# First stage of a two-layer diffusion backbone: pinning TensorE's order and rearranging what the pooling mixer waits for

## The chip, the cores and the metric

The kernel runs on one core of a Trainium2 chip. The metric is the device time of one execution in microseconds (us), as the median of several runs; lower is better. Engines are named as in the profile: PE is TensorE (matmuls), PEld its weight loads, DVE is VectorE, ACT is ScalarE, POOL is GpSimd, and SP is SyncE, which issues all the loads here. "Lnnn" is a line of the kernel before.

## The reference, cut to what matters

Two layers work on 512 latent tokens and 256 context tokens of width 1024, all in float32. Layer 0 mixes tokens by pooling, layer 1 by attention; each is followed by a squared-ReLU MLP with an inner width of 4096. Only the first half of layer 0 matters here:

```python
m = silu(cond) @ w_ada[i] + b_ada[i]             # 6 x 1024: sh1, sc1, gt1, sh2, sc2, gt2
h = rms_norm(x, g_mix_pre) * (1 + sc1) + sh1     # the context has its own conditioning vector
# pool_mixer, group g of four, window w = 2, 4, 8, 16 tokens
diff = mean_over_window(h) - h                   # the constant sh1 falls out of this difference
y    = concat(diff_g @ w_pool[g]) * pool_scale
x    = x + gt1 * rms_norm(y, g_mix_post)
h2   = rms_norm(x, g_mlp_pre) * (1 + sc2) + sh2
x    = x + gt2 * rms_norm(relu(h2 @ w_in) ** 2 @ w_out, g_mlp_post)
```

## The kernel before, in words

Matrix products are made in three passes of split operands: a "hi" copy rounded to the fp32r type and a "lo" remainder (hi·hi, hi·lo, lo·hi). So whatever enters a product has an ACT instruction that writes hi and a DVE instruction that writes lo. Tokens stand in six tiles of 128 rows: t = 0 to 3 latent, 4 and 5 context. Channels stand in eight blocks of 128: k = 0 to 7, two for each pooling group.

The first stage ends where the product of layer 0's `w_mlp_in` block 0 (`psin`, from tile `rb`) is done and that of block 1 (`psin` from tile `units`, L530) begins. It does the following.

1. SP issues the small `vecs` loads (L185, L186), the six row tiles and the band matrices (L189, L191), and then one block of 1 MB after another: twenty blocks of `w_ada` for layer 0 in the order of the list `CONDITIONING`, and `w_pool`. `raw_load` (L106 to L111) puts a block into a tile of a pool: `rawe` with four buffers unless another pool is given. SP waits until a buffer is free, and `keep_in_program_order` keeps the `raw_load`s in their order.
2. Row tiles: a mean square on ACT (L155), a power on POOL (L170), scaled rows on DVE (L314).
3. Pooling as a band matrix: `band_mm` (L394) multiplies rows by a band and writes the transposed difference of mean and row to PSUM, latent tokens in `psm`, context tokens in `psc`. `band_ev` (L405) copies blocks k = 0 to 3 to SBUF tiles `stage` of the pool `rawp` (three buffers); k = 4 to 7 stay in PSUM.
4. Conditioning: `ada_mm` (L200 to L211) multiplies the silu vector by a pair of blocks (w = 4, 512 columns) or one block (w = 2, 256 columns) on PE (L208) and transposes the result on DVE (L210). `ada_sel` (L218) sums it on PE (L215) and writes `mods` and `avec` on DVE (L226, L235). A buffer of `rawe` is free after L208, or, for the second block of a pair, after L215, because the transposed result is written into the block itself.
5. `centred(k)` (L422 to L433): the modulated difference, in hi and lo. It needs the shift and the scale of its blocks.
6. `pool_weights` (L441) loads `w_pool` into a `rawe` buffer and the scale row into a `rawp` tile, multiplies them on DVE (L446), and `split` (L124) makes hi and lo on ACT (L127) and DVE (L130).
7. `pool_a(t)` (L450): 24 matmuls into a PSUM tile of two banks from `psA`, which has two such tiles. `gate_rows` (L279) spreads the gate over the partitions on PE (L284) and copies it on ACT (L286). `pool_ms`, `pool_b` (L307), `norm_r` (L310), `norm_s`, `norm_c` make the residual and the scaled rows. `turn0`, `mod0` (L355 to L377) transpose and modulate them, and `parts0` runs `psin`.

Two things set the order. Each piece is put on a list with a planned time (`st.at(time, fn, ...)`, L690 to L737), and the list, sorted, gives the program order. The scheduler then orders each engine's instructions by its own estimate of when each is ready, with program order as priority, except for those in `keep_in_program_order`. On the chip each engine runs its instructions in the order that results. In the kernel before, no PE instruction of this stage is kept in program order.

## Time and profile before

| | |
|---|---|
| time, three runs | median 1180.1 us (1179.85 to 1182.94) |
| the profiled execution's own time | 1181.59 us |
| its span | 1179.8 us |
| PE busy over the span | 1143.2 us (97%) |
| DVE, ACT busy over the span | 941.9 us (80%), 639.2 us (54%) |
| mean granted TensorE clock | 0.993 |
| first product of block 1 (end of the first stage) | 111.08 us |

The span runs from the first instruction of the program to the last; the time holds 1.8 us more around it. A row of the timeline gives start, length, engine, line, operation, written<-read tiles, the number of instructions merged into it, and in brackets the idle time before it with what ended it. A row of the groups gives the number of instructions, the busy time and the mean in ns of one. A row of the stretches gives begin and end, length, then each engine's busy time and instructions, the granted TensorE clock as a share, the DMA engines' busy share and GB/s.

### The profile page before, as it was taken

What the parts mean: (1) busy time and instruction counts of PE and PEld (TensorE: products, weight loads), DVE (VectorE), ACT (ScalarE), POOL (GpSimd) and SP (SyncE); (2) the same over time, 40 slices, a digit from 0 to 9 for tenths busy, and PEclk for the clock granted to TensorE, in tenths of its full rate; (3) what the DMA queues carried; (4) which work ended last, traced back from release to release, by engine and by line L of the source; (5) the groups of instructions that cost most, each with busy time, mean ns of one, the idle gap of its engine ahead of it and who ended that gap; (6) DMA issues with size and microseconds to landing.
All of it is one profiled execution on the core that took longest, in us unless ns stands there. A gap on an engine that the chain in (4) does not pass through costs nothing.

```text
span 1179.8 us, 15965 instructions
## 1 busy us (share of the span) xinstructions
PE 1143.2 (97%) x6168; PEld 989.3 (84%) x6168; DVE 941.9 (80%) x1543; ACT 639.2 (54%) x1087; POOL 68.9 (6%) x120
## 2 busy tenths in 40 slices
PE   6799999999999999999999999999899999999997
PEld 4479989899889988998887889998888888888886
DVE  3777777989988999897687589977687779778876
ACT  3667654545444455554576377863676346535522
POOL 2030000000000000000131210001100000000001
PEclk9899999999999999999999999999999999999999
DMA  8986113443333343334521200105234124314212
GB/s 339 339 303 228 42 69 110 143 143 143 144 143 129 121 143 143 107 120 151 194 72 61 83 1 37 37 34 200 109 126 175 42 102 143 108 36 143 107 32 111
DMA packets 25658, 147.84 MB, mean 125 GB/s; under 512 B 2800, under 2 KB 5232, under 8 KB 9840
## 3 DMA queue, kind: packets, MB, share of 16 engines
q1 hardware_dynamic: 25584, 146.84, 34.6%
q8 instruction: 48, 0.79, 0.3%
q14 instruction: 26, 0.21, 0.1%
HBM read 139.49 MB, written 7.34 MB: 124 GB/s over the span
## 4 chain that ended last, share of the span: by engine, by line
PE 49%; issue 42%; DVE 3%; POOL 3%; ACT 2%; DMA 1%; SPq 0%; POOLq 0%; DVEq 0%; ACTq 0%
PE pso L758 22%; PE psin L654 18%; PE psin L530 3%; PE psq L1005 2%; PE pspool L457 2%; PE psada L208 1%; POOL rs L170 1%; ACT junk L155 1%; POOL rs L1014 1%; DMA xr<-in_x 1%; DVE xr L310 0%; PE psc L400 0%; PE psx L360 0%; DVE rows L250 0%; DVE ra L433 0%
## 5 line engine op out<-in xcount | busy, mean ns | idle before, releaser
L758 PE MATMUL pso<-units,rb 128*128 128x512 f32 x1152 | 278.2, 392 | 0.0
L758 PEld LDWEIGHTS pso<-units,rb 128*128 128x128 f32 x1152 | 214.8, 188 | 41.2
L250 DVE SCALAR_TENSOR_TENSOR rows<-raw,cond,rows 128x256 f32<-128x256 f32 x280 | 126.5, 477 | 2.0
L770 DVE TENSOR_TENSOR acc<-acc,pso 128x512 f32<-128x512 f32 x129 | 85.1, 675 | 40.8 <-PE pso L758 40.7
L530 PE MATMUL psin<-ra,rb 128*128 128x512 f32 (+1 forms) x432 | 104.0, 341 | 2.3 <-ACT ra L345 1.6
L862 PE MATMUL pso<-units,pairs 128*128 128x512 f32 x336 | 82.3, 389 | 0.0
L530 PEld LDWEIGHTS psin<-ra,rb 128*128 128x128 f32 x432 | 70.0, 189 | 12.6 <-ACT ra L345 1.9
L530 PE MATMUL psin<-ra 128*128 128x512 f32 x256 | 80.5, 389 | 0.0
L862 PEld LDWEIGHTS pso<-units,pairs 128*128 128x128 f32 x336 | 63.1, 188 | 13.1
L866 DVE TENSOR_TENSOR acc<-acc,pso 128x512 f32<-128x512 f32 x72 | 48.7, 683 | 28.5 <-PE pso L862 28.5
L168 POOL TENSOR_SCALAR ms<-ss 128x1 f32<-128x1 f32 x20 | 9.6, 480 | 1004.2 <-ACT junk L155 992.1
L654 PE MATMUL psin<-ra,units 128*128 128x384 f32 x336 | 65.6, 337 | 0.4 <-ACT psin L666 0.4
L654 PE MATMUL psin<-sums,units 128*128 128x384 f32 x336 | 63.9, 337 | 0.0
L654 PEld LDWEIGHTS psin<-ra,units 128*128 128x128 f32 x336 | 59.8, 188 | 4.0 <-ACT psin L666 0.9
L654 PEld LDWEIGHTS psin<-sums,units 128*128 128x128 f32 x336 | 58.9, 188 | 1.6
L130 DVE TENSOR_TENSOR units<-raw,units 128x1024 fp32r<-128x1024 f32 (+2 forms) x49 | 55.2, 1149 | 5.0 <-ACT units L127 4.9
L530 PEld LDWEIGHTS psin<-ra 128*128 128x128 f32 x256 | 48.0, 188 | 10.0
L768 ACT COPY acc<-pso 128x512 f32<-128x512 f32 x48 | 27.1, 587 | 50.0 <-PE pso L758 49.6
L127 ACT CAST units<-raw 128x1024 fp32r<-128x1024 f32 (+2 forms) x49 | 46.9, 994 | 13.2 <-PE pso L758 9.3
L530 PE MATMUL psin<-rb 128*128 128x512 f32 (+1 forms) x144 | 52.8, 367 | 0.2 <-DVE rb L346 0.2
L1005 PE MATMUL psq<-units,ra 128*128 128x512 f32 x216 | 51.7, 392 | 0.0
L530 PE MATMUL psin<-rb,ra 128*128 128x512 f32 x128 | 49.8, 389 | 0.0
(252 smaller groups left out, 2357.3 us busy)
## 6 DMA issues: line engine op xcount, KB each, us to landing
raw<-in_w_ada SPq DMA_DIRECT2D x48, 1024.0 KB, 5.3
raw<-in_w_mlp_in SPq DMA_DIRECT2D x32, 1024.0 KB, 4.9
raw<-in_w_mlp_out SPq DMA_DIRECT2D x32, 1024.0 KB, 5.3
raw<-in_w_qkv SPq DMA_DIRECT2D x6, 1024.0 KB, 4.9
spill<-xr SPq DMA_DIRECT2D x10, 512.0 KB, 6.2
xr<-spill SPq DMA_DIRECT2D x10, 512.0 KB, 7.8
raw<-in_w_o SPq DMA_DIRECT2D x4, 1024.0 KB, 5.0
xr<-in_x SPq DMA_DIRECT2D x4, 512.0 KB, 5.3
```

Of the source, the lines that this page charges most:

```text
L127: a = sc.copy(hi, raw)
L130: b = ve.tensor_tensor(out=lo, in0=raw, in1=hi, op=ALU.subtract)
L250: ve.scalar_tensor_tensor(out=r, in0=raw[:, k, :], scalar=cond[:, k, c:c + 1], in1=r, op0=ALU.mult, op1=ALU.add)
L457: te.matmul(pss[g // 2][:, (g % 2) * 256:(g % 2 + 1) * 256], a[:, k, sl], b[:, k, :], start=(n == 0), stop=(n == len(seq) - 1))
L530: te.matmul(ps[:, bank, o:o + ln], w[:, k, fs], rhs, start=start, stop=(k == KT - 1 and n == 2), skip_group_check=len(ks) < KT)
L654: te.matmul(bank, w[k], a[k], start=start and k == 0 and m == 0, stop=stop and k == 3 and m == 2, skip_group_check=True)
L758: te.matmul(pss[h][:, 0:cols[h][1]], a[:, f, ts_], w[:, f, cols[h][0]:sum(cols[h])], start=(n == 0 and not seeded[t]), stop=(n == len(seq) ...
L768: sc.copy(d, ps)
L770: ve.tensor_tensor(out=d, in0=d, in1=ps[:, 0:w], op=ALU.add)
L862: te.matmul(ps, a, w, start=(m == 0), stop=(m == len(seq) - 1))
L866: ve.tensor_tensor(out=M[n][:, t], in0=M[n][:, t], in1=ps, op=ALU.add)
L1005: te.matmul(ps, a[:, k, sl], w[:, k % 4, :], start=(k == 0 and n == 0), stop=(k == KT - 1 and n == 2))
```

## The change

It does six things, all in the first stage.

- **Order of PE.** A wrapper `Kept` around TensorE puts every PE instruction issued between the planned times 0 and 50.4 into `keep_in_program_order`. The planned times of the stage are set anew: `ada_mm` and `ada_sel` get a time each in place of one time and one more.
- **`vec`** is loaded after the rows instead of before them.
- **Pool weights.** `w_pool` goes to the pool `rawp`, not to a `rawe` buffer. The scale row is loaded in two halves into the unused 512 columns of the two `stage` tiles, and the multiplication is made in two halves (`pool_scaled`).
- **`centred` in two passes.** hi = scale·difference + 0 on ACT, lo = scale·difference − hi on DVE, straight from the difference. The separate product plus shift, and its subtraction, go. `minus` becomes a tile of zeros, computed as `mods − mods`, so that it still depends on the shift.
- **Mixer by groups.** `pool_a` can run some of the four groups: tiles 4 and 5 run groups 0 and 1, 2, and 3 at separate places, and tile 4 uses two one-bank tiles of the pool `psB` (four banks) instead of a `psA` tile.
- **Blocks of `band_mm`.** Blocks k = 4, 5 and 6, 7 go in pairs, latent tokens first.

```diff
+class Kept:
+    def __init__(self, tc, engine, on):
+        self.tc, self.engine, self.on = tc, engine, on
+    def __getattr__(self, name):
+        f = getattr(self.engine, name)
+        if not self.on[0]:
+            return f
+        return lambda *args, **kw: self.tc.keep_in_program_order(f(*args, **kw))
...
-    sy, ve, sc, gp, te = nc.sync, nc.vector, nc.scalar, nc.gpsimd, nc.tensor
+    ordered = [False]
+    sy, ve, sc, gp, te = nc.sync, nc.vector, nc.scalar, nc.gpsimd, Kept(tc, nc.tensor, ordered)
...
         if (i, m) == (0, SH1):
-            ve.tensor_scalar(out=minus[:, 2 * j:2 * j + w], in0=mods[i][:, at:at + w, 0:nc_], scalar1=-1.0,
-                             scalar2=None, op0=ALU.mult)
+            ve.tensor_tensor(out=minus[:, 2 * j:2 * j + w], in0=mods[i][:, at:at + w, 0:nc_],
+                             in1=mods[i][:, at:at + w, 0:nc_], op=ALU.subtract)
...
     def centred(k):
-        pm, w = means.pop(k), work_tile()
+        pm = means.pop(k)
         for ci, (t0, ln) in enumerate(SEGS):
-            z, hi, lo = w[:, t0:t0 + ln], hH[:, k, t0:t0 + ln], hL[:, k, t0:t0 + ln]
+            hi, lo, m = hH[:, k, t0:t0 + ln], hL[:, k, t0:t0 + ln], pm[ci][:, 0:ln]
             sa = avec[0][0][:, k, ci:ci + 1]
-            b = mods[0][:, SH1 * KT + k, ci:ci + 1]
-            if ci == 0:
-                sc.activation(z, pm[ci][:, 0:ln], AF.Identity, scale=sa, bias=b)
-            else:
-                ve.tensor_scalar(out=z, in0=pm[ci][:, 0:ln], scalar1=sa, scalar2=b, op0=ALU.mult, op1=ALU.add)
-            sc.activation(hi, z, AF.Identity, bias=minus[:, k, ci:ci + 1])
-            ve.scalar_tensor_tensor(out=lo, in0=z, scalar=b, in1=hi, op0=ALU.subtract, op1=ALU.subtract)
+            sc.activation(hi, m, AF.Identity, scale=sa, bias=minus[:, k, ci:ci + 1])
+            ve.scalar_tensor_tensor(out=lo, in0=m, scalar=sa, in1=hi, op0=ALU.mult, op1=ALU.subtract)
...
     def pool_weights():
-        wraw = raw_load(w_pool)
-        pscale = rawp.tile([P, 2048], F32, tag="raw", name="pscale")[:, 0:D]
-        sy.dma_start(pscale, pool_scale[0].partition_broadcast(P))
+        wraw = raw_load(w_pool, rawp)
         w4 = wraw.rearrange("p (g k n) -> p g k n", k=2, n=256)
-        ve.tensor_tensor(out=w4, in0=w4, in1=pscale.rearrange("p (g n) -> p g n", n=256).unsqueeze(2)
-                         .broadcast_to([P, 4, 2, 256]), op=ALU.mult)
-        pw.append((wraw, wpH, wpL))
-
-    def pool_a(t):
+        for h, (_, spare) in enumerate(stage.values()):
+            sy.dma_start(spare, pool_scale[0, 512 * h:512 * h + 512].partition_broadcast(P))
+        pw.extend((wraw, wpH, wpL))
...
+    def pool_a(t, gs=range(4), small_banks=False):
+        if t not in mix:
+            if small_banks:
+                mix[t] = [psB.tile([P, 512], F32, tag="b", name="pspool") for _ in range(2)]
+            else:
+                pp_ = psA.tile([P, 2, 512], F32, tag="a", name="pspool")
+                mix[t] = [pp_[:, 0, :], pp_[:, 1, :]]
         sl = slice(t * P, (t + 1) * P)
-        pp_ = psA.tile([P, 2, 512], F32, tag="a", name="pspool")
-        pss = [pp_[:, 0, :], pp_[:, 1, :]]
-        for g in range(4):
+        for g in gs:
...
-    landing = (15.3, 20.3, 26.2, 28.6, 31, 33.4, 39.5, 44.3, 49, 53.5, 58.5, 61, 63.4, 65.8)
-    for z, (m, j, w) in zip(landing, CONDITIONING):
-        ada_at(st, z, 0, m, j, w)
+    landing = ((19.5, 23.6), (21.5, 25.4), (28.4, 29.7), (30, 31.2), (32.5, 33.6), (35.2, 37.2), (42, 44.5), (47.2, 49.4),
+               (51, 53.2), (55.5, 57.6), (60.5, 61.7), (62.9, 64), (65.2, 66.4), (67.7, 68.8))
+    for (z, zs), (m, j, w) in zip(landing, CONDITIONING):
+        st.at(z, ada_mm, 0, m, j, w)
+        st.at(zs, ada_sel, 0, m, j)
+    st.at(0, ordered.__setitem__, 0, True)
+    st.at(50.4, ordered.__setitem__, 0, False)
...
-    for t in range(NT):
-        st.at(8 + 1.3 * t, band_mm, t, range(4))
+    for t, z in enumerate((8.6, 9.9, 11.3, 13, 14.6, 18.4)):
+        st.at(z, band_mm, t, range(4))
...
+    for k in (4, 6):
+        z = 16.1 if k == 4 else 23.4
+        st.at(z - 0.1, band_open, k)
+        for t in range(NL):
+            st.at(z + t / 10, band_mm, t, (k, k + 1))
+        for t in range(NL, NT):
+            st.at((25.6 if k == 4 else 27) + t / 10, band_mm, t, (k, k + 1))
     for k in range(KT):
-        st.at([22, 23.5, 25, 26.5, 30.2, 31.7, 35, 36.2][k], centred, k)
-    st.at(21.5, pool_weights)
-    st.at(27.5, lambda: split(*pw[0]))
+        st.at([26.4, 27.5, 28.6, 29.6, 32.2, 33.2, 38.2, 39.2][k], centred, k)
+    st.at(23, pool_weights)
+    st.at(25.3, pool_scaled)
+    st.at(30.5, lambda: split(*pw))
...
-            st.at((40.9, 45.7)[h] + (0.1, 0)[ci], gate_rows, 0, GT1, ci, (h,))
+            st.at((44.8, 49.6)[h] + (0.1, 0)[ci], gate_rows, 0, GT1, ci, (h,))
     order = (4, 5, 0, 1, 2, 3)
+    st.at(34.5, pool_a, 4, (0, 1), True)
+    st.at(36.7, pool_a, 4, (2,))
+    st.at(37.8, pool_a, 5, (0, 1, 2))
+    st.at(40.4, pool_a, 4, (3,))
+    st.at(40.5, pool_a, 5, (3,))
     for n, t in enumerate(order):
-        b = 46.4 + 3 * n
-        st.at((36.4, 39.8, 46.8, 49.8, 52.8, 55.8)[n], pool_a, t)
+        b = 50.5 + 2.9 * n
+        if n > 1:
+            st.at((44.9, 52.6, 55.6, 58.4)[n - 2], pool_a, t)
```

The planned times after these (`pool_ms`, `turn0`, `mod0`, `parts0`, the load of `w_mlp_in`) move later by 1.0 to 4.1 us.

More of the change, by code (lines that the diff above doesn't have):

```diff
@@ L185, in backbone @@
     sy.dma_start(given, vecs[:, 160:176])
-    sy.dma_start(vec, vecs[:, 0:160])
     xt = x.rearrange("b (t p) d -> p (b t) d", p=P)
@@ L193, in backbone @@
         xload(t)
+    sy.dma_start(vec, vecs[:, 0:160])
     sc.activation(cond[:, :, 0:2].rearrange("p k c -> p c k"), given.rearrange("p (c k) -> p c k", k=KT),
@@ L406, in band_ev @@
         if k not in stage:
-            stage[k] = rawp.tile([P, 2048], F32, tag="raw", name="stage")[:, 0:2 * TOK].rearrange("p (u n) -> p u n", n=TOK)
+            z = rawp.tile([P, 2048], F32, tag="raw", name="stage")
+            stage[k] = z[:, 0:2 * TOK].rearrange("p (u n) -> p u n", n=TOK), z[:, 2 * TOK:]
         t0, ln = SEGS[q]
-        (sc.copy if on_act else ve.tensor_copy)(stage[k][:, :, t0:t0 + ln], (lat, con)[q][k])
+        (sc.copy if on_act else ve.tensor_copy)(stage[k][0][:, :, t0:t0 + ln], (lat, con)[q][k])
         if q:
             for u in range(2):
-                means[k + u] = [stage[k][:, u, t0:t0 + ln] for t0, ln in SEGS]
+                means[k + u] = [stage[k][0][:, u, t0:t0 + ln] for t0, ln in SEGS]
     rs, mix, yg, first = {}, {}, {}, []
@@ L712, in backbone @@
[L712 to L713 removed]
+        st.at([26.4, 27.5, 28.6, 29.6, 32.2, 33.2, 38.2, 39.2][k], centred, k)
+    st.at(23, pool_weights)
+    st.at(25.3, pool_scaled)
+    st.at(30.5, lambda: split(*pw))
     raws = []
[L715 to L716 removed]
+    st.at(56.5, lambda: first.append(Inner(0, w_in(0, 0, ring, False, raws), hH, hL, hids0[0], chunks0, TOK)))
```

31 lines of the change are left out of this document (14 added, 17 removed).

## The prediction, made before the changed kernel was run

> **What bounds the kernel now.** I read the busy times by stretches first, then PE's waits, SP's issues and landings, and the timeline of PE and DVE in the stretch with the idle time.
>
> ```profile
> 0.00:28.60 28.60, 19.67 (x136) 14.58 (x136) 9.22 (x20) 11.49 (x18) 7.61 (x18) 1.00 0.89 336
> 28.60:44.60 16.00, 7.62 (x93) 3.27 (x89) 14.67 (x29) 11.93 (x19) 0.00 (x0) 0.75 0.99 367
> 44.60:65.60 21.00, 19.18 (x165) 13.69 (x161) 11.67 (x28) 8.88 (x20) 1.72 (x4) 0.86 0.91 340
> 65.60:111.20 45.60, 44.39 (x421) 37.94 (x418) 35.11 (x60) 31.85 (x61) 12.41 (x20) 1.00 0.67 245
> 111.20:150.00 38.80, 38.80 (x203) 35.87 (x202) 30.98 (x42) 28.04 (x40) 0.00 (x0) 1.00 0.22 80
> ```
>
> Columns: stretch, length, PE, PEld, DVE, ACT, POOL busy, granted clock, DMA share, GB/s. From 65.6 on PE is the bound: 44.39 of 45.6 us, then 38.8 of 38.8. So the kernel gains what the first stage lets PE reach earlier. The idle time lies before: 8.4 us of 16 from 28.6 to 44.6, where DVE is busy for 14.67 us, and the clock is 0.75 there and 0.86 in the next stretch.
>
> ```profile
> PE psada L208 <- DMA raw<-in_w_ada: 4.1, 2, 3.6
> PE psada L215 <- DVE mods L226: 3.4, 1, 3.4
> ```
>
> In this stretch (waits of PE, 26 to 45 us) PE waits for a block of `w_ada`, then, at L215, for DVE. Why is that block late?
>
> ```profile
> 1.63 0.42 SPq L189 DMA_DIRECT2D xr<-in_x  x1
> 4.95 2.82 SPq L108 DMA_DIRECT2D raw<-in_w_ada  x4
> 22.23 0.33 SPq L108 DMA_DIRECT2D raw<-in_w_pool  x1
> 26.50 23.32 SPq L108 DMA_DIRECT2D raw<-in_w_ada  x9
> raw<-in_w_ada SPq DMA_DIRECT2D x1, 1024.0 KB, 10.1
> raw<-in_w_ada SPq DMA_DIRECT2D x1, 1024.0 KB, 15.0
> pscale<-in_pool_scale SPq DMA_DIRECT2D x1, 512.0 KB, 13.9
> raw<-in_w_pool SPq DMA_DIRECT2D x1, 1024.0 KB, 7.7
> raw<-in_w_ada SPq DMA_DIRECT2D x1, 1024.0 KB, 6.6
> ```
>
> The last column of the DMA rows is us from issue to landing: for the first and fourth of the four early blocks (issued at 4.95 and 7.44), for the scale row (11.28), `w_pool` (22.23) and the next `w_ada` (26.50). So blocks land at 15.05 and 22.44, (22.44 − 15.05) / 3 = 2.46 us each; scale row and gains at 25.2; `w_pool` only at 29.9, because its `rawe` buffer came free at 22.2; the next `w_ada` at 33.1, where PE's wait ends.
>
> **The change part by part.** I follow PE up to the gate.
>
> ```profile
> 8.63 6.11 PE L400 MATMUL psm<-gate,acc 128*128 128x136 f32 x32 [8.63 <-DVE acc L314]
> 15.03 1.19 PE L400 MATMUL psc<-gate,acc 128*128 128x136 f32 x8 [0.30 <-DVE acc L314]
> 16.06 3.02 PE L400 MATMUL psm<-gate,acc 128*128 128x136 f32 x24
> 48.39 1.90 PE L208 MATMUL psada<-raw,cond 128*32 128x512 f32 x16
> 59.38 0.25 PE L215 MATMUL psada<-raw,sel 128*32 128x8 f32 x8 [1.22 <-DVE raw L210]
> 50.36 0.72 DVE L210 STREAM_TRANSPOSE raw<-psada 128x512 f32<-128x512 f32 x1 [0.48 <-PE psada L208]
> 53.64 0.23 DVE L273 TENSOR_TENSOR gc<-mods,vec 128x4 f32<-128x4 f32 x2
> 53.30 1.22 PE L457 MATMUL pspool<-rb,ra 128*128 128x256 f32 x8
> 54.36 1.95 PE L284 MATMUL psg<-ident,gc 128*128 128x128 f32 x16
> 60.21 3.45 PE L284 MATMUL psg<-ident,gc 128*128 128x128 f32 x16 [0.58 <-DVE gc L273]
> 63.69 0.58 ACT L286 COPY gate<-psg 128x512 f32<-128x512 f32 x1 [1.12 <-PE psg L284]
> 65.60 6.01 PE L457 MATMUL pspool<-rb,ra 128*128 128x256 f32 x48
> ```
>
> *`vec` behind the rows* frees one SP issue ahead of them: the rows' first issue moves from 1.63 to 1.16, and all that follows with it, PE's start at 8.63 too: 0.47 us. The `w_ada` blocks behind `vec` gain less; I take 22.2 for the fourth.
>
> *PE's order up to 25.7.* Tile 4 starts at 15.03 − 0.47 = 14.6 and ends at 15.8; 16 instructions for k = 4, 5 at 3.02 / 24 = 0.126 take 2.0, tile 5 takes 1.2: 19.0. Then the first pair, 1.9: 20.9. The second pair's first half, 0.95, ends at 21.85, its second waits for 22.2: 23.15. The latent k = 6, 7, 2.0: 25.2; two sums at 0.25: 25.7. Scale and shift are there at about 26.5 and `centred` begins, against 30.04 (first L429) before. The bands of the context fill PE until 28.1.
>
> *Pool weights out of `rawe`.* SP issues `w_pool` right behind the fourth block: 22.2 + 2.5 = 24.7. Scale row and gains took 25.2 − 22.44 = 2.8 before and are still there: 27.5. The first `rawe` buffer comes free at 19.9, halfway through the first pair, and goes to `w_ada` at once; the next at 21.85 and, behind the two sums, about 25.5. So the next four blocks land at 30.0, 32.4, 34.9 and 37.4, against 33.1 and on: three us earlier. If the scale's halves went behind a `w_ada` block, they would land 2.5 later; DVE has `centred` to do meanwhile, so I count nothing. The Trainium skill, "DMA: Bandwidth & Descriptors", section Bandwidth, has a rule that speaks against this part: transfers should be of 1 MiB or more, and the halves have a quarter of that. By the fixed 2.0 us that the page puts on each transfer, the scale would be about 2 us later, an estimate; the trace shows landings 2.46 us apart in a queue of blocks, with no such gap between them, and the sum stays either way, as `centred` fills DVE.
>
> *`centred` in two passes, and DVE's sum.* The next bound is DVE:
>
> ```profile
> L433 DVE SCALAR_TENSOR_TENSOR ra<-work,mods,ra 128x512 fp32r<-128x512 f32 x8 | 6.0, 745 | 0.1
> L433 DVE SCALAR_TENSOR_TENSOR ra<-work,mods,ra 128x256 fp32r<-128x256 f32 x8 | 3.7, 469 | 0.0
> L431 DVE TENSOR_SCALAR work<-psc,avec,mods 128x256 f32<-128x256 f32 x4 | 2.0, 538 | 0.0
> L431 DVE TENSOR_SCALAR work<-stage,avec,mods 128x256 f32<-128x256 f32 x4 | 1.5, 406 | 0.0
> L446 DVE TENSOR_TENSOR raw<-raw,pscale 128x2048 f32<-128x2048 f32 x1 | 2.3, 2284 | 0.0
> L130 DVE TENSOR_TENSOR rb<-raw,rb 128x2048 fp32r<-128x2048 f32 x2 | 4.6, 2292 | 0.0
> L210 DVE STREAM_TRANSPOSE rows<-psada 128x256 f32<-128x256 f32 x8 | 3.5, 442 | 0.6 <-PE psada L208 0.5
> L226 DVE TENSOR_TENSOR mods<-psada,vec 128x4 f32<-128x4 f32 x8 | 1.2, 155 | 3.2 <-PE psada L215 3.1
> L307 DVE TENSOR_TENSOR acc<-pspool,gate 128x512 f32<-128x512 f32 x12 | 7.8, 682 | 8.8 <-ACT gate L286 5.0 <-ACT junk L155 3.8
> L429 ACT ACTIVATE work<-psm,mods,avec 128x512 f32<-128x512 f32 x4 | 2.9, 773 | 6.5 <-DVE mods L226 6.5
> ```
>
> Gone are the eight of L431, 4 × 0.538 + 4 × 0.406 = 3.8 us of DVE, and the eight of L429 on ACT, 8 × 0.79 = 6.3 us, which were not the bound. Left from 26.5 on: 16 lo's, 8 × (0.745 + 0.469) = 9.7; scaling 2.28; split 2.29; four transposes 1.77; eight small ones 1.25: 17.3 us, so DVE is through at 43.8 if nothing starves it. The last conditioning needed, at 37.4, is then no bound. A lo with its source in PSUM has no row; by L307, which reads PSUM, a 512 one lies near 0.68, by L433 at 0.745, so 16 of them change the sum by under 0.6; I keep L433.
>
> *Mixer by groups.* The same 24 instructions for a tile, at 6.01 / 48 = 0.125. Only the last group of tiles 4 and 5, 12 × 0.125 = 1.5, is left after 43.8: 45.3. Before, these tiles ended at 53.30 + 1.22 = 54.5: 9.2 earlier. Two banks of `psB` are held until `pool_b`; two are left for conditioning and gate, which go one after another. Nothing by that, and up to one gate copy, 0.58, if they collide.
>
> *From there to the gate, pinned.* The first gate pair (in by 42.4) 1.9: 47.2; transpose 0.72, sum 0.25, `mods` and gate column 0.155 + 0.23: 48.6; `psg` 1.95: 50.5; `pool_a(0)` 24 × 0.125 = 3.0: 53.5; second pair (in by 47.4) 55.4; the same 1.37: 56.8; `psg` 58.7; second gate copy about 59.5, against 63.69 + 0.58 = 64.3. The scheduler can put the first SC2 pair, 1.9, under the copies: PE is at 60.9 where it was at 65.6, with `pool_a(0)` done besides. In this walk PE stands idle for two transposes, sums and small ones, 2 × 1.1 us; nothing ready may pass a pinned instruction.
>
> *After 60.9* the same work is left less 3.0 us: 45.6 − 3.0 = 42.6, so the stage ends at 103.5 in place of 111.2. The blocks of SC2 and SH2 come some 11 us earlier than before by the same chain of buffers, so they don't bound it; DVE has 35.1 us of work in it and ACT 31.9, still under 42.6. The gain is (65.6 − 60.9) + 3.0 = **7.7 us**. The profiled execution, 1181.6, becomes 1173.9; it lies 1.5 over the median of 1180.1, which becomes **1172.4**.
>
> **The rivals.**
>
> *A. The stream of blocks sets the end.* DVE gets through sooner (small ones under other waits, the split early), and the gate follows its block. Then the second gate pair at 47.4 gives the gate after 0.95 + 1.37 + 1.95 + 0.58 at 52.3, and PE, with `pool_a(0)` still ahead, gains about 12: 1168. For it: DMA share 0.99 in the second stretch. Against it: DVE's sum above, and `pool_a(0)` pinned between the pairs.
>
> *B. The clock stays low.*
>
> ```profile
> 37.50:40.90 3.40, 0.01 (x2) 0.01 (x2) 3.38 (x5) 1.32 (x3) 0.00 (x0) 0.88 1.03 371
> 40.90:44.60 3.70, 3.70 (x41) 1.63 (x41) 2.88 (x9) 3.15 (x6) 0.00 (x0) 0.50 1.00 376
> ```
>
> After 3.4 us of idle PE runs at 0.50 for the next 3.7. My walk uses warm durations. If short waits keep it cold from 43.8 on, `pool_a(0)` costs 3.0 more, and the first `psg` 1.5 (3.45 against 1.95; the second was cold before as well, so its 1.5 is a gain that my walk counts and this case does not get): gain 7.7 − 6.0 = 1.7, or up to 4 if it is cold for part of the way; 1177 in the middle. Against it: my gaps are 2.4 us at most. The Trainium skill, "TensorE: Matmul & The Clock Gate", Part 1, puts the drop to half after an idle window of about 3.4 us and the return after as long a busy one; the two rows agree, and by that rule gaps of 2.4 keep the clock.
>
> *C. Slower: the pinned queue waits for DVE.* L215 is now a gate in PE's queue, and the L210 before it stands in DVE's queue behind lo's (0.745), scaling and split (2.3 each). The trace has one such wait, 3.4 us (L215 <- DVE mods above). Four sums stand pinned between 28 and 40; the buffers, so the blocks, wait behind them, and shift and scale too. Four uncovered ones cost 13.6: 1172.4 + 13.6 = 1186. It decides from 7.7 / 3.4 = 2.3 of them. Against it: DVE is the bound in that stretch anyhow, so PE's waits there are mostly covered.
>
> The order of PE can't fail to be pinned; but after 50.4 the scheduler is free, and it may place the tail worse than before, by a few us.
>
> **How the numbers follow.** Forecast, gain 4.5 to 11: 0.55. A: 0.18. B, gain −1 to 4.5: 0.15. C: 0.12. About 0.3%, 3.5 us, is what a measurement of this kernel can tell from no change. Faster is the forecast, A and the upper fifth of B, 0.55 + 0.18 + 0.03 = 0.76; the same is the rest of B, and C's mildest, 0.13; slower 0.11. The range goes from A with 2 us more, 1166, to no gain, 1180.5; it leaves out C and a tail of A.
>
> **What would show it.** Right: `w_pool` landing near 25, the next `w_ada` near 30; no L429 and no L431; tiles 4 and 5 done near 45; last gate copy near 59.5; `psin` of block 1 near 103.5. Wrong: PE waiting at L215 for DVE for more than 2 us at a time; a clock under 0.8 between 44 and 60; `psin` work after 60 with idle time of more than 3 us.

## The result, and the profile after

The changed kernel takes 1182.75 us (median; 1181.42 to 1184.75), the kernel before 1180.29 us beside it (1178.58 to 1184.06); the ratio is 1.0016 with a 95% interval of 1.0007 to 1.0024. Forecast were 1172.4 us and a range of 1166 to 1180.5: the prediction is wrong, by 10 us and on the other side. Executions of one kernel scatter by 3 to 6 us here, in step with the clock that they were granted (last section), so I go by the stage in the traces first and by medians second. The profiled execution of e5 below had a granted clock of 0.87 on average and took 1245 us, so its trace gives no times of the stage.

In the trace of the changed kernel (span 1179.97 us, own time 1181.75) the first product of block 1, the end of the stage, stands at 110.68 us, against 111.08 before and 103.5 forecast. From there to the end of the span it takes 1069.3 us, against 1068.7. So nearly all of the expected gain is missing inside the stage. Its busy times by stretches, in the columns of the prediction:

```profile
28.60:44.60 16.00, 8.09 (x86) 4.68 (x86) 12.82 (x24) 7.96 (x12) 0.00 (x0) 0.66 1.00 409
44.60:65.60 21.00, 17.56 (x153) 11.99 (x153) 6.58 (x17) 6.39 (x14) 1.72 (x4) 0.93 0.51 184
65.60:111.20 45.60, 44.33 (x427) 37.02 (x427) 38.18 (x64) 35.42 (x66) 9.85 (x20) 1.00 0.77 294
```

The reader is to see three things. PE is idle for 7.9 us of the first stretch, hardly less than before, and its clock fell further, to 0.66. DVE, which the forecast took to be full there, has 12.82 of 16 us, and then 6.58 of 21. And in the second stretch the DMA engines are busy for half of the time only (0.91 before): blocks wait for free buffers (from 20 to 66 us SP's longest wait for a product of PE is 7.0).

What PE waits for between 28.6 and 60 us (all pinned PE instructions have line L65, that of the wrapper, so one goes by tiles; us in total, times, longest; two waits of 0.5 and 0.2 us are left out):

```profile
PE psada L65 <- DVE rows L224: 5.1, 3, 3.3
PE psada L65 <- DMA raw<-in_w_ada: 2.8, 1, 2.8
PE psada L65 <- DVE raw L224: 0.8, 1, 0.8
PE psg L65 <- DVE gc L287: 0.6, 1, 0.6
```

L224 is the transpose of a conditioning product, which the sum behind it needs. This is the sign that the prediction named for "wrong". The timeline of PE shows what stands behind these waits:

```profile
31.72 1.07 PE L65 MATMUL psada<-raw,cond 128*32 128x256 f32 x16 [2.78 <-DMA raw<-in_w_ada]
36.12 0.29 PE L65 MATMUL psada<-rows,sel 128*32 128x4 f32 x8 [3.33 <-DVE rows L224]
36.24 1.93 PE L65 MATMUL psada<-raw,cond 128*32 128x256 f32 x16
38.92 0.29 PE L65 MATMUL psada<-rows,sel 128*32 128x4 f32 x8 [0.74 <-DVE rows L224]
39.05 1.93 PE L65 MATMUL psada<-raw,cond 128*32 128x256 f32 x16
42.04 0.29 PE L65 MATMUL psada<-rows,sel 128*32 128x4 f32 x8 [1.06 <-DVE rows L224]
42.26 2.93 PE L65 MATMUL pspool<-rb,ra 128*128 128x256 f32 x12
45.12 1.94 PE L65 MATMUL psada<-raw,cond 128*32 128x256 f32 x16
```

Rows `raw,cond` are products, rows `rows,sel` the sums. Product, sum, product, sum: each product begins the moment the sum ahead of it is done, though its block lies there already. The last one, for the second half of the shift, starts at 45.12; its block landed at 39.0. And on DVE:

```profile
25.73 0.23 DVE L989 TENSOR_SCALAR grow<-grow 128x128 f32<-128x128 f32 x1 [4.17 <-DMA grow<-in_g_q]
25.87 0.71 DVE L224 STREAM_TRANSPOSE raw<-psada 128x512 f32<-128x512 f32 x1
...
29.11 2.36 DVE L461 TENSOR_TENSOR raw<-raw,stage 128x1024 f32<-128x1024 f32 x2 [1.79 <-DMA raw<-in_w_pool]
31.39 4.31 DVE L443 SCALAR_TENSOR_TENSOR ra<-stage,avec,ra 128x512 fp32r<-128x512 f32 x8
35.62 0.44 DVE L224 STREAM_TRANSPOSE rows<-psada 128x256 f32<-128x256 f32 x1
35.99 2.25 DVE L144 TENSOR_TENSOR rb<-raw,rb 128x2048 fp32r<-128x2048 f32 x1
...
47.12 0.45 DVE L224 STREAM_TRANSPOSE rows<-psada 128x256 f32<-128x256 f32 x1 [3.76 <-PE psada L65]
```

Here the other half of the lock is seen. DVE too runs in order. A small one first: the gains (L989) wait for their load, and a transpose whose product was done at 23.7 waits behind them until 25.87. The scaling (L461) waits for `w_pool`, with the eight lo's (L443) behind it and the transpose behind those: the product that it transposes was done at 32.8, the transpose runs at 35.62. Then, at 47.12, DVE has waited 3.76 us for the product that stood pinned behind a sum and twelve pool matmuls. Each engine waits for the other in turn.

Why `w_pool` is late is seen on SP (issues, then KB and us from issue to landing):

```profile
5.43 3.47 SPq L122 DMA_DIRECT2D raw<-in_w_ada  x4
9.85 0.33 SPq L455 DMA_DIRECT2D stage<-in_pool_scale  x1
11.13 0.33 SPq L987 DMA_DIRECT2D grow<-in_g_q  x1
12.42 0.33 SPq L988 DMA_DIRECT2D grow<-in_g_k  x1
12.79 0.43 SPq L455 DMA_DIRECT2D stage<-in_pool_scale  x1
15.11 0.33 SPq L122 DMA_DIRECT2D raw<-in_w_pool  x1
```

```profile
raw<-in_w_pool SPq DMA_DIRECT2D x1, 1024.0 KB, 14.0
```

It was issued behind the scale's halves and the gains, not ahead of them, and landed at 15.11 + 14.0 = 29.1. The DMA rate from 20 to 30 us, in 40 slices of 0.25 us, shows what those small loads cost:

```profile
GB/s 328 492 459 492 393 246 402 336 299 174 27 72 49 66 123 193 234 320 379 428 526 414 352 418 418 426 459 393 393 426 393 524 426 393 393 393 492 492 360 393
```

From 22.25 to 24 us, the halves and gains, the rate falls from about 300 to between 27 and 193 GB/s. Between the fourth block (landed 22.59) and the last half (26.61) lie 4.0 us, against 2.8 for the same bytes in one scale row before. The Trainium skill, "DMA: Bandwidth & Descriptors", section Bandwidth, advises transfers of 1 MiB or more. The prediction set that aside; these 1.2 us go its way. The fixed 2.0 us per transfer that the prediction took from the same page of the Trainium skill stands there for loads that GpSimd issues. SP issues these, and splitting the row cost 1.2.

### The profile page after: what moved, and what is told of

The parts are those of the page before. It is cut to its first block, busy times and chain, and to the rows that moved or that the text cites. A ratio compares the mean times of both kernels' runs of the same rounds, so it can differ in the third digit from the quotient of the medians.

```text
span 1180.0 us, 15950 instructions
## 1 busy us (share of the span) xinstructions
PE 1140.9 (97%) x6168; PEld 988.1 (84%) x6168; DVE 938.0 (79%) x1536; ACT 635.1 (54%) x1079; POOL 65.8 (6%) x120
## 3 DMA queue, kind: packets, MB, share of 16 engines
q1 hardware_dynamic: 25728, 146.84, 33.9%
## 5 line engine op out<-in xcount | busy, mean ns | idle before, releaser
L672 PEld LDWEIGHTS psin<-sums,units 128*128 128x128 f32 x336 | 58.9, 188 | 1.6
L141 ACT CAST units<-raw 128x1024 fp32r<-128x1024 f32 (+2 forms) x49 | 46.8, 994 | 13.7 <-PE pso L787 9.6
L548 PE MATMUL psin<-rb 128*128 128x512 f32 (+1 forms) x144 | 52.8, 367 | 0.2 <-DVE rb L360 0.2
L548 PE MATMUL psin<-rb,ra 128*128 128x512 f32 x128 | 49.8, 389 | 0.0
```

What stands on the lines that cost most here:

```text
L141: a = sc.copy(hi, raw)
L548: te.matmul(ps[:, bank, o:o + ln], w[:, k, fs], rhs, start=start, stop=(k == KT - 1 and n == 2), skip_group_check=len(ks) < KT)
L672: te.matmul(bank, w[k], a[k], start=start and k == 0 and m == 0, stop=stop and k == 3 and m == 2, skip_group_check=True)
```

## The experiments

**T**, my theory: the pinned order is a chain. Each sum in PE's queue waits for a transpose that stands in DVE's queue behind scaling, lo's or split; each product and pool group stands behind that sum; the next DVE work, the buffers and so the blocks wait behind those. **Rivals**: *R*, the pool weights land late, and that alone set the stage; *DVE's sum*, the prediction's own bound; *the clock*, which is 0.50 from 33.7 to 47.4 us. No run changes the clock alone.

All runs in one table. "Tiles": the last pool matmul of tiles 4 and 5. "Gate": the last gate copy. "Block 1": its first product, the stage's end. "Rest": from there to the end of the span. All in us of the trace. "Median" is the time; the ratio is that to the kernel before, run beside each (medians 1179.6 to 1180.3), as its 95% interval. The times of a stage come from one execution each. In changed, e1, e2, e4, e6, e13 and e14, whose first loads are the same, `w_pool` landed between 28.6 and 30.0, so differences of about a us between two stages can be chance.

| run | tiles | gate | block 1 | rest | median | ratio |
|---|---|---|---|---|---|---|
| before | 54.5 | 64.3 | 111.1 | 1068.7 | 1180.3 | |
| changed | 53.5 | 68.0 | 110.7 | 1069.3 | 1182.8 | 1.0007 to 1.0024 |
| e1 no pin | 52.8 | 63.6 | 108.2 | 1068.9 | 1179.4 | 0.9980 to 1.0001 |
| e2 products first | 52.3 | 66.8 | 109.5 | 1069.6 | 1180.8 | 0.9986 to 1.0010 |
| e3 weights first | 50.2 | 64.7 | 107.5 | 1071.1 | 1180.9 | 0.9987 to 1.0017 |
| e4 three passes | 54.0 | 68.6 | 111.3 | 1068.9 | 1181.3 | 0.9994 to 1.0016 |
| e5 pin to 28 | | | | | 1179.8 | 0.9980 to 0.9998 |
| e6 loosened | 53.8 | 64.8 | 107.5 | 1069.5 | 1178.0 | 0.9964 to 0.9985 |
| e7 before, two passes | 55.3 | 63.4 | 109.4 | 1068.8 | 1179.7 | 0.9985 to 1.0006 |
| e8 weights first, no pin | 50.9 | 62.2 | 105.1 | 1068.8 | 1174.6 | 0.9933 to 0.9961 |
| e9 weights first, loosened | 48.8 | 60.6 | 103.3 | 1071.0 | 1175.1 | 0.9941 to 0.9967 |
| e10 before, weights first | 50.6 | 58.9 | 104.5 | 1069.2 | 1177.3 | 0.9964 to 0.9986 |
| e11 e10, two passes | 50.5 | 58.6 | 104.3 | 1068.9 | 1175.5 | 0.9955 to 0.9979 |
| e12 e8, whole tiles | 53.6 | 62.6 | 108.3 | 1070.3 | 1179.0 | 0.9978 to 0.9995 |
| e13 scaling behind | 53.9 | 68.4 | 111.8 | 1069.5 | 1184.9 | 1.0027 to 1.0053 |
| e14 e13, loosened | 51.6 | 62.6 | 106.9 | 1070.4 | 1180.0 | 0.9990 to 1.0009 |
| e15 e9, second sum first | 49.5 | 60.0 | 104.0 | 1068.8 | 1175.7 | 0.9953 to 0.9977 |

**e1, no pin.**

```diff
-    st.at(0, ordered.__setitem__, 0, True)
+    st.at(0, ordered.__setitem__, 0, False)
```

> The changed kernel without the pin: every PE instruction is left to the scheduler, all else as changed. Theory T (the pinned queue is a chain: each ada_sel waits for a DVE transpose that stands behind scaling, lo's and split, and each next ada_mm stands behind that ada_sel; so the block of SH1 3, landed at 39.0 us, is multiplied at 45.1) expects the four small products nearer to their landings, tiles 4 and 5 done about 49 to 51 instead of 53.5, and 2 to 4 us less than the changed kernel. Rival R (the pool weights alone: they land at 29.1 and DVE scales them ahead of the lo's) expects no change, within 1 us of the changed kernel, as the weights land at 29.1 here too.

2.5 us of the stage come back, and 3.4 us of the median: the pinned order costs time. (The planned times are the same, but DVE's order moves with PE's: here two lo's run ahead of the scaling.) It does not cost it where T said. The last two products start at 39.08 and 45.52, against 39.05 and 45.12 pinned, the last lo ends at 52.57 against 52.33, and the tiles are 0.7 us earlier, where T expected 2.5 to 4.5. What came back lies behind: the first gate product stood pinned behind the tiles in the changed kernel (first row) and ran ahead of their end in e1 (second row), and the last gate copy came 4.4 us earlier.

```profile
53.41 1.93 PE L65 MATMUL psada<-raw,cond 128*32 128x512 f32 x16
48.79 1.92 PE L222 MATMUL psada<-raw,cond 128*32 128x512 f32 x16 [0.28 <-DVE mods L240]
```

**e2, products first.** Still pinned; the product for the shift goes ahead of the sum for the scale, in both pairs.

```diff
-    landing = (... (28.4, 29.7), (30, 31.2), (32.5, 33.6), (35.2, 37.2), ...
+    landing = (... (28.4, 31), (30, 31.2), (32.5, 34.1), (33, 37.2), ...
```

> The changed kernel, pinned, with the four small products moved ahead of the sums of their neighbours (SC1 2, SH1 2, then both sums; SC1 3, SH1 3, then both sums); DVE's and SP's order as changed but for the transposes. Theory T expects SH1 3 multiplied at about 40 instead of 45.1, tiles 4 and 5 done at 48 to 49 instead of 53.5, and 3 to 5 us less than the changed kernel. Rival R expects the first sum still at 36.1 and everything behind it, within 1 us.

The last product ran at 40.1 instead of 45.1, as T says, but the tiles were done only 1.2 us earlier, where T expected 48 to 49. Its sum stood pinned behind 18 pool matmuls until 46.8, though its transpose was done at 43.0. The chain closed one link further on. The median fell by 1.9, where T expected 3 to 5.

**e3, weights first.** Still pinned; `w_pool` and the whole scale row are loaded ahead of the conditioning, scaled and split early.

```diff
-        for h, (_, spare) in enumerate(stage.values()):
-            sy.dma_start(spare, pool_scale[0, 512 * h:512 * h + 512].partition_broadcast(P))
+        pscale = work_tile()
+        tc.keep_in_program_order(sy.dma_start(pscale, pool_scale[0].partition_broadcast(P)))
...
-    st.at(23, pool_weights)
-    st.at(25.3, pool_scaled)
-    st.at(30.5, lambda: split(*pw))
+    st.at(4, pool_weights)
+    st.at(16.9, pool_scaled)
+    st.at(19.2, lambda: split(*pw[:3]))
```

> The changed kernel, pinned, with w_pool and its scale loaded ahead of the conditioning (the scale into a free work tile), scaled and split while DVE is idle before 25 us. The first conditioning then lands some 4 us later, the later blocks at the same time as before. Theory T expects the first transpose to be on time, the sum of SC1 2 at 33 to 34 instead of 36.1, the chain after it as it was: 3 to 5 us less than the changed kernel. Rival R expects the whole forecast gain: DVE through at about 44, 7 to 8 us less than the changed kernel.

3.2 us of the stage, within T's 3 to 5, though the first two conditioning pairs now land at 18.9 to 26.4, 3.8 us later. The first sum came at 35.3, later than T's 33 to 34. So the weights are a loss of their own beside the pin, and neither T nor R has it all. The median shows only 1.8 of it: "rest" is 1.8 us longer, for which see the last section.

**e4, three passes.** The changed kernel with `centred` and `minus` as before.

```diff
-            sc.activation(hi, m, AF.Identity, scale=sa, bias=minus[:, k, ci:ci + 1])
-            ve.scalar_tensor_tensor(out=lo, in0=m, scalar=sa, in1=hi, op0=ALU.mult, op1=ALU.subtract)
+            if ci == 0:
+                sc.activation(z, pm[ci][:, 0:ln], AF.Identity, scale=sa, bias=b)
+            else:
+                ve.tensor_scalar(out=z, in0=pm[ci][:, 0:ln], scalar1=sa, scalar2=b, op0=ALU.mult, op1=ALU.add)
+            sc.activation(hi, z, AF.Identity, bias=minus[:, k, ci:ci + 1])
+            ve.scalar_tensor_tensor(out=lo, in0=z, scalar=b, in1=hi, op0=ALU.subtract, op1=ALU.subtract)
```

> The changed kernel with the old centred: the scaled and shifted difference is written first, hi and lo come from it. That adds 3.8 us of DVE and 6.3 us of ACT work to the stretch from 27 to 52 us. If DVE's sum bounds that stretch, as the prediction had it, the time rises by 3.8 us. Theory T, for which DVE is idle for 8 to 9 us in that stretch because it waits for the pinned chain, expects 1 to 2 us more than the changed kernel, as only what lies between one sum and the next is in the chain.

DVE has 3.8 us more to do, and the stage ends 0.6 us later, with `w_pool` landing 0.9 later too; the median is not longer (1181.3), where T expected 1 to 2 us more. DVE's sum is not the bound. The work disappears in DVE's waits.

**e5, pinned only up to 28.** 

```diff
-    st.at(50.4, ordered.__setitem__, 0, False)
+    st.at(28.2, ordered.__setitem__, 0, False)
```

> The changed kernel with PE kept in program order only up to the planned time 28.2 instead of 50.4; all planned times as in the changed kernel. T (the pinned queue is a chain: each sum waits for a DVE transpose, and what stands behind it waits too; all such waits lie after 28): about as with no pin at all, tiles 4 and 5 done 51 to 53, last gate copy 62 to 64.5, first product of block 1 at 107 to 109, 1178.3 to 1180. Rival P (the pin harms by what it does before 28: late load of the pool weights, first pairs): nothing is won, first product of block 1 at 110 to 111, 1181.5 to 1183.

1179.8, within T's range and near e1: what the pin costs, it costs behind 28. Rival P falls. Whether at the sums or at the gate's products this time does not say; e1 speaks for the latter.

**e6, the chain loosened.** Pinned to 50.4; sums go where their transposes are done, the gate's products ahead of pool groups.

```diff
-    (28.4, 29.7), (30, 31.2), (32.5, 33.6), (35.2, 37.2), (42, 44.5), (47.2, 49.4),
+    (28.4, 31), (30, 31.2), (32.5, 34.1), (33, 34.4), (37.9, 40.6), (40.7, 45.2),
```

> The changed kernel, pinned to 50.4 as it is, but with sums placed where their transposes are done: first sum of SC1 2 after the product of SH1 2, the sum of SH1 3 ahead of the pool groups, the first gate product ahead of the last pool groups, the second ahead of the mixer of tile 0. T: PE waits for DVE shrink to under 1 us, the sum of SH1 3 near 43 (46.8 with the products alone moved), tiles 4 and 5 done 47 to 50.5, last gate copy 59.5 to 63, first product of block 1 at 102.5 to 106, 1174.5 to 1178. Rival R (the pool weights' late landing and the scaling ahead of the lo's set the stage): no better than with the products alone moved, last gate copy 66 to 67, block 1 at 109 to 109.8, 1180 to 1181. Rival clock (half clock from 36 to 47 is the loss): tiles 4 and 5 done 51 to 52.5, block 1 at 107 to 109.

The time is at the upper end of T's range (1178.0), the stage 1.5 us short of it; PE still waits up to 2.2 us for DVE, where T expected under 1, and the tiles are not earlier. The last conditioning sum came at 44.1, a us later than expected, and the last lo ended 2.5 us earlier than in the changed kernel (49.8); but all pool groups stand behind that sum now, and PE, idle up to 32 and again before 35 and 39, runs at half clock from 33.9 to 47.6. The gate is 3.2 us earlier, as its first product went ahead of the last pool groups. The clock's rival had block 1 at 107 to 109, which holds, and the tiles at 51 to 52.5, which does not. Pool matmuls of e6, and of e9 where PE has no such gaps:

```profile
44.28 6.00 PE L65 MATMUL pspool<-rb,ra 128*128 128x256 f32 x36
```

```profile
40.78 4.57 PE L65 MATMUL pspool<-rb,ra 128*128 128x256 f32 x36
```

So the half clock is worth 1.4 us in these 36 matmuls: a part of the loss, and by its place behind PE's waits a consequence of them.

**e7, two passes alone.** The kernel before with the new `centred` and `minus`, nothing else (the same lines as in the change).

> The kernel before with nothing but the centred rows in two passes. The sum of the prediction (DVE bounds the stretch up to tiles 4 and 5): 3.8 us less of DVE's work, tiles 4 and 5 done near 50.7 instead of 54.5, first product of block 1 near 107.3, 1176 to 1177. T (DVE's sum is not the bound, products, sums and landings are): tiles 4 and 5 done 52.5 to 54.3, block 1 at 109 to 111, 1178 to 1180.

1179.7; the prediction's sum asked for 1176 to 1177. The tiles were done even later (55.3, later than T's range too), and the stage ended 1.7 us earlier, where the sum asked for 3.8. DVE's sum was not the bound in the kernel before either, full as it looked with 14.67 of 16 us.

**e8, weights first and no pin**: the edits of e1 and e3 together.

> The kernel with the pool weights loaded, scaled and split ahead of the conditioning, and no pin. T: both gains add in part, tiles 4 and 5 done 48 to 50.5, last gate copy 60 to 63, first product of block 1 at 104 to 107, 1175 to 1178.5. Rival R (the pool weights alone were the loss): the same as with the pool weights first and the pin, block 1 at 107 to 108, 1179.5 to 1181.

1174.6, the lowest median here. Stage: 2.5 from e1 and 3.2 from e3 make 5.7; measured 5.6. The two losses add.

**e9, weights first and loosened**: the edits of e3 and e6.

> The loosened chain (sums placed where their transposes are done, gate products ahead) together with the pool weights loaded, scaled and split ahead of the conditioning; PE pinned to 50.4. T (what the change lost is the chain in the pinned queue, and the pool weights that stand in DVE's queue ahead of it): both out of the way, tiles 4 and 5 done 47 to 51, last gate copy 60 to 63, first product of block 1 at 103 to 106, 1173 to 1176.5. Rival P (a pinned order costs by itself, however it is laid): 2 us or more over the same weights without the pin, block 1 at 107 or later, 1177 or more.

A pinned order need not harm: block 1 begins at 103.3, 1.8 us before e8's, and PE waits for DVE at the sums twice, 1.1 us at most. That the prediction had 103.5 is in part luck: the tiles were done 3.5 us after its 45.3 and the gate 1.1 after its 59.5.

```profile
28.60:44.60 16.00, 13.11 (x176) 10.84 (x176) 10.89 (x32) 9.94 (x18) 0.00 (x0) 0.98 0.98 386
44.60:65.60 21.00, 19.29 (x171) 13.25 (x169) 10.01 (x19) 7.87 (x18) 2.94 (x8) 1.00 0.89 348
```

PE does 13.11 us of work in the first stretch instead of 8.09, at a clock of 0.98 instead of 0.66, with *less* of DVE (10.89). Where scaling and split went, the timeline of DVE in e9 shows:

```profile
16.30 2.29 DVE L459 TENSOR_TENSOR raw<-raw,work 128x2048 f32<-128x2048 f32 x1
...
20.56 2.29 DVE L144 TENSOR_TENSOR rb<-raw,rb 128x2048 fp32r<-128x2048 f32 x1 [1.36 <-ACT rb L141]
```

They run where DVE waits for conditioning anyway.

**e10, the kernel before, weights first**; **e11**, the same with two passes.

```diff
-        wraw = raw_load(w_pool)
-        pscale = rawp.tile([P, 2048], F32, tag="raw", name="pscale")[:, 0:D]
-        sy.dma_start(pscale, pool_scale[0].partition_broadcast(P))
+        wraw = raw_load(w_pool, rawp)
+        pscale = work_tile()
+        tc.keep_in_program_order(sy.dma_start(pscale, pool_scale[0].partition_broadcast(P)))
...
-    st.at(21.5, pool_weights)
-    st.at(27.5, lambda: split(*pw[0]))
+    st.at(4, pool_weights)
+    st.at(16.9, pool_scaled)
+    st.at(19.2, lambda: split(*pw[0]))
```

> The kernel before with nothing but the pool weights and their scale row loaded, scaled and split ahead of the conditioning. W (the weights' late landing and the scaling held the lo's in the kernel before too): tiles 4 and 5 done 50 to 52.5, first product of block 1 at 106 to 109, 1175 to 1178.5. Its rival (the blocks of w_ada, which now land 3.9 us later for the first pairs, set that stretch): tiles 4 and 5 done 53.5 to 56, block 1 at 110 to 113, 1179 to 1182.

> The same with the centred rows in two passes. If DVE's work bounds the stretch once the weights are early: another 2 to 4 us below the weights first alone, tiles 4 and 5 done 47 to 50. If sums and landings do: under 1 us below it.

Without any pin, group or new pass, the early weights alone take 6.6 us off the stage of the kernel before, more than W expected: W holds and its rival falls. The median fell by 2.7 only (1180.0 to 1177.3): the profiled execution of the kernel before lies 1.6 above its median and that of e10 1.6 below its own. So part of the 6.6 belongs to these two executions, and 2.7 is what the time shows. The two passes then add 0.2 us of the stage. The medians lie 1.8 apart, but within the scatter (e10 1175.7 to 1179.7, e11 1174.8 to 1177.8), so I take the stage.

**e12, whole tiles**: e8 with tiles 4 and 5 of the mixer in one piece.

```diff
-    st.at(34.5, pool_a, 4, (0, 1), True)
-    st.at(36.7, pool_a, 4, (2,))
-    st.at(37.8, pool_a, 5, (0, 1, 2))
-    st.at(40.4, pool_a, 4, (3,))
-    st.at(40.5, pool_a, 5, (3,))
+    st.at(39.8, pool_a, 4)
+    st.at(40.5, pool_a, 5)
```

> Pool weights first and no pin, as in the run at 1174.6, but tiles 4 and 5 of the mixer whole and behind the last centred rows, in psA tiles as in the kernel before. If the groups are worth what the prediction gave them (half of the 48 products moved under other waits, and the mixer of tile 0 ahead of the gate): tiles 4 and 5 done 2 to 4 us later, the mixer of tile 0 behind the gate copies, block 1 at 107 to 109.5, 1176.5 to 1179. If PE has time to spare there anyhow: 104.5 to 106.5, 1174 to 1176.

3.2 us of the stage and 4.4 of the median are lost: the groups, with their places and the banks of `psB` that go with them, are worth about what the prediction gave them, once something feeds them.

**e13, scaling behind the lo's**: the changed kernel, same loads, with the first eight lo's and the scaling kept in this order on DVE; **e14**, the same with e6.

```diff
+            if k < 4:
+                tc.keep_in_program_order(z)     # z: the lo of L443
...
-            ve.tensor_tensor(out=w4[:, 2 * h:2 * h + 2], ...
+            tc.keep_in_program_order(ve.tensor_tensor(out=w4[:, 2 * h:2 * h + 2], ...
...
-    st.at(25.3, pool_scaled)
-    st.at(30.5, lambda: split(*pw))
+    st.at(29.9, pool_scaled)
+    st.at(31.9, lambda: split(*pw))
```

> The changed kernel, pinned as it is and with the same loads, but the scaling of the pool weights kept behind the first eight lo's in DVE's queue. D (the scaling stood in DVE's queue, waiting for its late weights, with the lo's and so every transpose behind it): lo's from 26.6 instead of 31.4, first sum of SC1 2 at 33.5 to 34.5 instead of 36.1, the chain shifts by that, tiles 4 and 5 done 51 to 52, first product of block 1 at 108.3 to 109.3, 1179.5 to 1181. N (the place in the queue is indifferent, since scaling and split have to be done before the first pool group): 110.2 or later, 1181.5 to 1183.

> The same with the loosened chain. If the place in DVE's queue and the chain in PE's queue are two separate losses: tiles 4 and 5 done 50.5 to 52.5, first product of block 1 at 104.5 to 106.3, 1175.5 to 1177.5. If they are one and the same: as with the loosened chain alone, 107 to 108, 1177.5 to 1178.5.

D falls. The lo's began at 28.1 and the first sum came at 33.6, both near D's numbers, and the stage ended at 111.8, not earlier than with the scaling ahead (110.7). The median, 1184.9, lies above what either side expected. DVE in e13, and the sums of PE in e13:

```profile
35.82 2.36 DVE L463 TENSOR_TENSOR raw<-raw,stage 128x1024 f32<-128x1024 f32 x2
38.09 0.44 DVE L224 STREAM_TRANSPOSE rows<-psada 128x256 f32<-128x256 f32 x1
...
40.14 2.29 DVE L144 TENSOR_TENSOR rb<-raw,rb 128x2048 fp32r<-128x2048 f32 x1 [0.83 <-ACT rb L141]
42.35 0.74 DVE L443 SCALAR_TENSOR_TENSOR ra<-psm,avec,ra 128x512 fp32r<-128x512 f32 x1
43.01 0.44 DVE L224 STREAM_TRANSPOSE rows<-psada 128x256 f32<-128x256 f32 x1
```

```profile
38.59 0.29 PE L65 MATMUL psada<-rows,sel 128*32 128x4 f32 x8 [2.22 <-DVE rows L224]
38.72 1.93 PE L65 MATMUL psada<-raw,cond 128*32 128x256 f32 x16
43.50 0.29 PE L65 MATMUL psada<-rows,sel 128*32 128x4 f32 x8 [2.86 <-DVE rows L224]
```

The scaling moved from ahead of the first transpose to ahead of the second, and the split to ahead of the third: the wait of 3.33 us became waits of 2.22 and 2.86. This is T in its plainest form: in a chain it doesn't matter which link carries the 4.6 us, and the tiles were done at 53.9 instead of 53.5. Loosened as well (e14), the stage ends 0.6 us before e6, between the two expectations, with `w_pool` landing 1.2 us earlier: no sign of a second, separate loss. (Its median, 1180.0, is 2.0 above e6's; its trace has the late clock drop of the last section, that of e6 has not.)

**e15, second sum first**: e9 with the sum of the second gate product ahead of the mixer of tile 0 (`(40.7, 44.85)` for `(40.7, 45.2)`).

> The loosened chain with the pool weights first, and the sum of the second gate product ahead of the mixer of tile 0. If the gate's copies are still what the rest waits for: last gate copy 56.5 to 59 instead of 60.6, first product of block 1 at 101 to 102.8, 1172.5 to 1174.5. If PE's work from there on is the bound, and the mixer of tile 0 only changes its place: 103 to 103.8, 1174.5 to 1176.

The gate was done 0.7 us earlier and block 1 began 0.7 later. But this trace has a stretch at half clock inside the stage that e9 has not:

```profile
78.25:81.66 3.41, 3.41 (x30) 1.92 (x23) 3.41 (x9) 2.87 (x6) 1.37 (x4) 0.50 0.97 398
```

It costs up to 1.7 us, so by itself the earlier sum may have gained up to 1.0, and this run does not settle the question. PE is busy for 42.65 of the 44.08 us from the gate to block 1, which speaks for PE's own work as the bound there, as the prediction had it.

## Why the prediction was wrong, point by point

- *`vec` behind the rows*: right in the issue, which moved from 1.63 to 1.15; but PE's start, which was to move as much, moved from 8.63 to 8.45 only.
- *PE's order up to 25.7*: right to 1.2 us; the two sums ran at 25.3 and 26.6, forecast done by 25.7.
- *Pool weights out of `rawe`*: wrong in its order. "SP issues `w_pool` right behind the fourth block: 22.2 + 2.5 = 24.7" became 29.1: 2.8 us because scale and gains went ahead, 1.2 because the halves are slow, 0.4 because the fourth block came at 22.6. The next blocks landed at 31.6, 34.1, 36.5 and 39.0, 1.6 us late each.
- ***`centred` in two passes, and DVE's sum*: the step that failed.** Left are 17.3 us, "so DVE is through at 43.8 if nothing starves it". The work was right; DVE was starved:

```profile
26.50:52.33 25.83, 17.12 (x161) 11.56 (x161) 16.51 (x36) 12.30 (x19) 0.00 (x0) 0.74 0.85 340
L443 DVE SCALAR_TENSOR_TENSOR ra<-psm,avec,ra 128x512 fp32r<-128x512 f32 x4 | 3.0, 751 | 2.2 <-ACT ra L442 2.1
L443 DVE SCALAR_TENSOR_TENSOR ra<-stage,avec,ra 128x512 fp32r<-128x512 f32 x4 | 3.0, 743 | 0.0
```

  The last lo ended at 52.33. From 26.5 until then DVE did 16.51 us of work (a lo from PSUM takes 751 ns, from SBUF 743, as assumed) and was idle for 25.83 − 16.51 = 9.3: 3.8 waiting for a product on PE, 2.1 for the hi's on ACT, 1.8 for `w_pool`, 1.2 for sums on PE. The lo's were 8.5 us late, tiles 4 and 5 8.2 us, and the end of the stage 7.2: the whole miss of the stage is there. A sum of durations is a bound only if the work is ready when its turn comes; mine had left out that DVE's transposes feed PE and PE's sums feed DVE, both in fixed order. e4 shows that the sum was no bound here, and e7 that it was none before.

  The bound in its place was the chain from the landing of the last of the four small blocks, through product, transpose, sum and hi, to the end of the last lo. The forecast has 43.8 − 37.4 = 6.4 us for it, the changed kernel 52.33 − 39.03 = 13.3: of the 8.5 us, 1.6 are the late landing and 6.9 this chain. It took 12.9 in e1 (no pin), 12.4 in e2, 10.1 in e6 (order loosened), 10.1 in e3 (weights first), 9.7 in e8 (weights first, no pin) and 6.9 in e9 (both). So the order as it was laid and the scaling and split inside the chain cost 3.2 us each and 6.4 together; dropping the pin without another order gave 0.4. The half clock goes along with the waits in these runs and is not separated.
- "DVE has `centred` to do meanwhile", the cover for a late scale row: wrong here, since scaling stood *ahead* of the lo's in DVE's queue; but e13 shows that having it behind them buys nothing.
- *Mixer by groups*: right where its inputs come (e12: 3.2 us, with places and banks).
- *From there to the gate*: right. 14.2 us from the tiles to the last gate copy were forecast, 68.0 − 53.5 = 14.5 measured.
- *After 60.9*: right (the walk's own 58.7 + 1.9 makes 60.6, 0.3 less than it went on with); 42.6 us forecast from there to the end, 43.4 measured (67.29 to 110.68).
- *Rival C*, with a chance of 0.12, came nearest. Its price was counted in the wrong place. The waits at the sums come to 5.1 us where it asked for 13.6; what stands behind them (a product 6 us behind its block, DVE idle 3.76 behind that) comes on top, and by e1 the pin itself cost 2.5 us of the stage, most of it behind the tiles. My argument against it, that DVE is the bound there anyhow, rested on the failed sum. *Rival B* took part, earlier than it said: the clock was 0.50 from 33.7 to 47.4. Its argument against itself fails too: by the Trainium skill's rule as the prediction used it, gaps of 2.4 us keep the clock, and here it fell at 33.7 with no gap of PE ahead of it longer than 2.8. Nor do its two rows show the return after 3.4 us of work: in the kernel before PE worked from 40.9 on and the clock was back at 46.9.
- The scale: of the 10.3 us between 1172.4 and 1182.75, 7.2 are the stage's, 0.6 the rest of the span's, and 2.5 come from the two profiled executions, of which that of before lies 1.5 above the forecast's median and that of after 1.0 below its own.

## What to carry to other kernels

Before adding up an engine's work as a bound, follow one item through all the engines that it crosses: if two in-order queues feed each other, the end is set by the chain of hand-overs, and taking work off one of them gains little (e7: 1.7 us of 3.8 in the stage, e11: 0.2). In an order pinned on one engine, each consumer needs enough other ready work ahead of it to cover its producer's queue on the other. Work that depends on nothing late, here the scaling and splitting of weights, belongs in the stretch where its engine waits anyway: moved there alone it took 6.6 us off the stage of the kernel before in one trace each, and 2.7 off the median (e10).

## What the runs showed of the hardware that I had not expected

**The scatter goes with the clock, and a late drop of it is a part.** "Rest" in the table falls into two groups, 1068.7 to 1069.6 and 1070.3 to 1071.1. In the traces with the longer one (e3, e9, e12, e14) the clock drops once near 840 to 850 us. That stretch in e8 and in e9:

```profile
840.00:850.00 10.00, 9.10 (x61) 8.34 (x62) 8.90 (x11) 8.46 (x13) 0.00 (x0) 1.00 0.26 89
```

```profile
840.00:850.00 10.00, 9.78 (x59) 9.15 (x58) 7.43 (x9) 6.99 (x11) 0.00 (x0) 0.83 0.30 105
```

Both kernels have the same waits of PE there (833 to 850 us, the rows are the same in both):

```profile
PE psin L545 <- ACT ra L359: 1.6, 1, 1.6
PE psx L345 <- DVE acc L506: 1.6, 1, 1.6
```

A clock of 0.83 over 10 us is 1.7 us lost. So two kernels with the same gaps, 1.6 us each, get the drop or not. The Trainium skill, "TensorE: Matmul & The Clock Gate", Part 1, has the clock halved after an idle window of about 3.4 us, and calls that window free-running; the second agrees with the chance seen here, the first does not by itself explain a drop at gaps of 1.6 us. In all four traces the clock falls after 6.83 us in which PE was busy for just under half, 3.37 or 3.38 us; in e9:

```profile
834.85:841.68 6.83, 3.38 (x26) 2.90 (x26) 4.76 (x9) 4.61 (x9) 0.71 (x2) 1.00 0.11 43
```

And every stretch at half clock in these traces but the last one of each lasts 3.41 us or a multiple of it, up to 17.07 (e5's trace set aside). What sets the drop is not shown. The drop is a likely reason why e9's median is not below e8's though its stage is 1.8 us shorter. The scatter as a whole goes with the clock: of the 35 executions of the kernel before that were timed beside e1 to e4, the 24 up to 1180.7 have a mean granted clock of 0.993 or 0.994, the 11 above 1181.6 one of 0.989 to 0.992. That the drop near 845 us is the one that these had is not shown: only one execution of each kernel has a trace.

**Small loads in the stream.** Two loads of 256 KB and two of 64 KB took 4.0 us of the stream, in which blocks of 1 MB land 2.5 us apart.
